# A deeper look ahead at the first double pair of each feed-forward

## The chip, the cores and the metric

One core of a Trainium2 chip runs the whole kernel. The metric is the device time in microseconds of one execution; the number given is the median of several runs. The engines named are TensorE (PE; its weight loads PEld), VectorE (DVE), ScalarE (ACT), GpSimd (POOL) and SyncE (SP), which here only issues transfers.

## The reference, cut to what matters

One decoder block on 512 tokens of width 1024, all in float32: a gated feed-forward, a token-mixing layer (pooling and dilated attention), a second gated feed-forward, each with a normalisation whose shift, scale and gate come from a small conditioning product.

```python
def swiglu(u, w_in, w_out):
    a, b = jnp.split(u @ w_in, 2, axis=-1)
    return (jax.nn.silu(a) * b) @ w_out

u = modulate(rmsnorm(h, g_norm_ffn1[l]), sh1, sc1)
h = h + 0.5 * gt1 * swiglu(u, w_ffn1_in[l], w_ffn1_out[l])
...
h = h + 0.5 * gt3 * swiglu(u, w_ffn2_in[l], w_ffn2_out[l])
return rmsnorm(h, g_final)
```

The hidden width is 2816, that is 22 tiles of 128; each needs two columns of tiles of `w_in`, one for `a` and one for `b`. The change lies in the two feed-forwards alone.

## The kernel before, in words

**Numbers in two parts.** Every weight and activation is held as a high part, rounded to the fast matmul type (`fp32r`), and a low part, the rest. A product is three matmuls: high by high, high by low, low by high (`mm3`, L356).

**Chunks.** The weights come in chunks, mostly 128 x 1024 numbers (512 KB). `plan` (L150) lists them in the order of use. SyncE loads a chunk into one of five buffers (`fetch`, L227; the names are raw, and X for the buffers that lie in another tile). Then ScalarE writes its high part to `whi` (L313) and VectorE the low part to `wlo` (L327). For some chunks (`self.outer`) the low part is made another way: ScalarE writes the negative of the rounded chunk to `wlo` (L309), and an accumulating transfer that GpSimd issues (L311) adds the chunk from HBM. `whi` and `wlo` are rings with room for seven chunks (RING, L121, a little over 7 x 1024 columns); `room` (L259) says whether a chunk fits beside those still in use.

**The look ahead.** Ahead of each chunk's matmuls, `look(n)` (L336) fetches what it has buffers for and splits chunks up to n places ahead, as far as the ring has room. The schedule is manual: each engine executes its instructions in exactly the order in which this Python code issues them, so where `look` stands, and how far it looks, fixes where a piece stands among ScalarE's and VectorE's other work.

**The feed-forward.** Its first hidden tiles are computed plainly (`ffn_pair`, L710, and, in the second feed-forward, written out in `ffn2`, L928): one tile for `a`, one for `b`, each 8 x 3 matmuls on one chunk. From hidden tile 8 on (first feed-forward) or 4 on (second), two hidden tiles at a time are made by a scheme of seven products of half-size blocks in place of eight: the double pair, `duo` (L773). Some of its chunks are differences of loaded ones (`make`, L246, VectorE, L252), and some of its inputs sums of activations (the tiles S). Between its products ScalarE copies partial sums out of the accumulation banks (L776) and takes the silu (L794). The first double pair of each feed-forward also calls `first` behind its first product, which makes the last sum (L733 on ScalarE, L736 on VectorE) and then gives a buffer free. The second matrix is applied in the same way, four hidden tiles at a time: `out_quad` (L869), with its own copies on ScalarE (L873) and sums of hidden activations made by `h_sums` (L843: VectorE L853 and L859, ScalarE L856), which `later` and `step` drop in between the double pair's products. Both loops count seven products; a product here is 24 matmuls of 256 columns.

In the first feed-forward the order is: plain tiles 6 and 7, the double pair of 8 and 9, a quad, two double pairs, a quad, and so on. In the second: plain tiles 0 to 3, the double pair of 4 and 5, a quad, and so on. Look-ahead before: 4 in the last plain tiles, 3 to 5 within the first double pair, 5 in all later double pairs and quads.

Of the kernel before, what the change touches and what calls it, by code (L numbers as in the profile page):

```python
# [125 lines left out]
PLAIN = {0: 8, 2: 4}  # L126
# [16 lines left out]
class Kernel:  # L143
# [272 lines left out]
    def beside(self, j, i):  # L416

        if self.nh == 4 and j > PLAIN[0] and i in (2, 5):
            self.bg()
# [290 lines left out]
    def ffn_pair(self, j, beside=lambda: None):  # L710
        ahead = 3 + (j + 2 >= PLAIN[0])
        pa = self.ffn_tile(ahead)
        beside()
        s = self.ffn_silu(j, pa)
        pb = self.ffn_tile(ahead)
        beside()
        self.ffn_post(j, s, pb)

# [54 lines left out]
    def duo(self, j, first, last):  # L773

        nc, v = self.nc, self.nc.vector
        copy = lambda o, x: nc.scalar.activation(o, x, AF.Copy)  # L776
        T1, T2 = slice(0, HT), slice(HT, T)
        blk = lambda ks, t: [(self.UH[k][:, t], self.UL[k][:, t]) for k in ks]
        lo4, hi4 = range(4), range(4, 8)
        S = []  # L780
        for i in range(3):
            h, l = self.S[i]
            S.append([(h[:, k * HT:(k + 1) * HT], l[:, k * HT:(k + 1) * HT]) for k in range(4)])
        S.append(blk(lo4, T2))
        A, B, C = self.nb(), self.nb(), self.nb()
        s = self.fw.tile([P, 2 * T], F32, name="sl")
        q = lambda x: x.rearrange("p (j h t) -> p j h t", j=2, h=2)
        r = lambda x: x.rearrange("p (j t) -> p j t", j=2)
        u3 = r(self.fw.tile([P, T], F32, name="u3"))
        c = self.kept[j // 2 % 3]  # L790
        c0, c1 = q(c)[:, :, 0, :], q(c)[:, :, 1, :]
        ts = slice(0, 1 if j % 4 == 0 and j < PARTS[-1][0] else 2)
        HHp, HLp = (q(x) for x in self.hpair(j))
        silu = lambda h, bank: nc.scalar.activation(q(s)[:, :, h, :], r(bank), AF.Silu)  # L794

        def mult():
            v.tensor_tensor(c, s, c, op=OP.mult)

        def high():
            copy(HHp[:, :, ts, :], q(c)[:, :, ts, :])  # L800

        def low():
            v.tensor_tensor(HLp[:, :, ts, :], q(c)[:, :, ts, :], HHp[:, :, ts, :], op=OP.subtract)


        for i, (bank, u, start) in enumerate(((A, blk(lo4, T1), True), (B, S[0], True), (A, S[1], False),
                                              (C, blk(hi4, T1), False), (A, S[2], False), (B, S[3], False),
                                              (A, blk(hi4, T2), False))):
            if i == 6:
                v.tensor_tensor(c1, c1, u3, op=OP.add)  # L810
            self.look(3 + i // 3 if first else 5)
            self.product(bank, u, start)
            self.step()
            if i == 0:
                copy(C, A)
                if first:
                    first()
                    self.free.append(self.rawx[0])
            elif i == 1:
                copy(c1, r(B))  # L820
            elif i == 2:
                copy(c0, r(A))
            elif i == 3:
                silu(0, C)
            elif i == 4:
                copy(u3, r(A))
            elif i == 6:
                silu(1, A)
                v.tensor_tensor(c0, r(B), c0, op=OP.add)
            self.beside(j, i)  # L830
            if self.nh == 4 and j > PARTS[-1][0] and self.todo:
                self.todo.pop(0)()
        if last:
            mult()
            high()
            low()
        else:
            self.later(1, mult)
            n = 8 if self.nh == 4 and j % 4 == 0 else 2
            self.later(n, high)  # L840
            self.later(n, low)
# [86 lines left out]
    def ffn2(self):  # L928
        self.put, self.now = [], 0
        bk = [self.nb() for _ in range(4)]  # L930
        self.head(2, bk, AF.Silu)
        self.open_G()
        self.todo, last = self.u_steps(2)
        do = lambda n: [self.todo.pop(0)() for _ in range(n)]
        do(3)
        for j in range(2):
            self.ffn_post(j, self.ffn_silu(j, bk[2 * j]), bk[2 * j + 1], lambda low: (do(1), low()))
        pa = self.ffn_tile()
        do(len(self.todo))
        self.free.append(self.rawx[1])  # L940
        due = []
        self.ffn_post(2, self.ffn_silu(2, pa), self.ffn_tile(), due.append)
        pa = self.ffn_tile(4)
        due.pop()()
        self.ffn_post(3, self.ffn_silu(3, pa), self.ffn_tile(4), lambda low: self.later(1, low))
        self.ffn(2, 4, last)

    def open_G(self):
# [779 lines left out]
```

## Time and profile before

| | us |
|---|---|
| median of 3 runs | 1002.2 (1002.18 to 1004.14) |
| the profiled execution | 1001.14 |
| its span, first to last instruction | 999.4 |
| TensorE busy | 984.8 |
| VectorE busy | 807.2 |
| ScalarE busy | 544.9 |
| granted TensorE clock, mean | 0.998 |

Times in rows of the profile are microseconds from the span's start. A row of the timeline gives start, duration, engine, line, operation, what it writes and reads, shapes, count, and in brackets the idle time of that engine ahead of it with what ended it. The ends of matmuls are modelled, their starts are measured. The first double pair of the first feed-forward starts at 125.83 (L769), its quad at 145.16 (L891); in the second feed-forward the quad starts at 722.11.

### The profile page before, as it was taken

The page shows a single profiled execution, that of the slowest core. Times are in us where ns is not written, and L with a number is a line of the kernel's source. Part 1 is how long each engine was busy: PE and PEld are TensorE (multiplying, and loading weights), DVE is VectorE, ACT ScalarE, POOL GpSimd, SP SyncE. Part 2 cuts the span into 40 slices and gives each one's busy share as a digit, 9 for nine tenths or more (in the row PEclk, how much of TensorE's full clock was granted, in tenths as well). Part 3 has the DMA queues.
Part 4 walks back from the last instruction along what each step waited for, and adds up shares of the span by engine and source line. Part 5 has one row for each costly group of instructions (what it writes and reads, how often), then busy time and mean ns, then how long its engine had stood idle before and what let it go on. Part 6 is the DMA issues. An engine that isn't in the chain of part 4 may idle for free.

```text
span 999.4 us, 17017 instructions
## 1 busy us (share of the span) xinstructions
PE 984.8 (99%) x6868; PEld 915.4 (92%) x6868; DVE 807.2 (81%) x1229; ACT 544.9 (55%) x824; POOL 67.0 (7%) x75
## 2 busy tenths in 40 slices
PE   8999999999999999999999999999999999999997
PEld 6888899999999999889988888898999999999996
DVE  6979979999996677879567777569798989989654
ACT  6453277786766443333414233465577868676652
POOL 0000001110110000007100000000010110010001
PEclk9999999999999999999999999999999999999999
DMA  9867567867857223123265774323376567567502
GB/s 338 278 212 251 190 169 211 222 184 216 241 126 198 89 78 106 57 92 125 77 235 185 266 267 133 96 73 106 111 169 192 143 171 179 156 151 204 137 17 85
DMA packets 49601, 163.29 MB, mean 163 GB/s; under 512 B 5617, under 2 KB 8945, under 8 KB 49522
## 3 DMA queue, kind: packets, MB, share of 16 engines
q1 hardware_dynamic: 42354, 137.95, 40.5%
q0 software_dynamic: 6480, 23.60, 14.2%
q8 instruction: 54, 0.88, 0.4%
q10 hardware_dynamic: 688, 0.66, 0.2%
q14 instruction: 25, 0.20, 0.1%
HBM read 159.41 MB, written 2.77 MB: 162 GB/s over the span
## 4 chain that ended last, share of the span: by engine, by line
PE 94%; DVE 3%; DMA 1%; ACT 1%; issue 1%; DVEq 0%; ACTq 0%; POOLq 0%
PE bank L358 13%; PE bank L359 13%; PE bank L360 13%; PE bank L771 10%; PE bank L769 10%; PE bank L770 10%; PE bank L891 4%; PE bank L893 4%; PE bank L892 4%; PE bank L1658 2%; PE bank L1662 1%; PE bank L1660 1%; PE bank L1249 1%; DMA wlo<-wf1o 1%; PE bank L1430 1%; PE bank L1431 1%
## 5 line engine op out<-in xcount | busy, mean ns | idle before, releaser
L327 DVE TENSOR_TENSOR wlo<-raw,whi 128x1024 fp32r<-128x1024 f32 (+5 forms) x129 | 140.3, 1099 | 45.3 <-ACT whi L313 45.1
L313 ACT ACTIVATE whi<-raw 128x1024 fp32r<-128x1024 f32 (+5 forms) x157 | 148.1, 955 | 18.9 <-DMA raw<-wmix 6.3
L358 PE MATMUL bank<-UH,whi 128*128 128x512 f32 (+1 forms) x432 | 158.1, 366 | 0.0
L359 PE MATMUL bank<-UL,whi 128*128 128x512 f32 (+1 forms) x432 | 154.0, 357 | 0.1
L360 PE MATMUL bank<-UH,wlo 128*128 128x512 f32 (+1 forms) x432 | 153.9, 356 | 0.0
L771 PE MATMUL bank<-UH,wlo 128*128 128x256 f32 x512 | 141.4, 276 | 0.0
L769 PE MATMUL bank<-UH,whi 128*128 128x256 f32 x512 | 141.4, 276 | 0.0
L770 PE MATMUL bank<-UL,whi 128*128 128x256 f32 x512 | 141.4, 276 | 0.0
L769 PE MATMUL bank<-SH,whi 128*128 128x256 f32 x384 | 107.0, 279 | 0.0
L771 PE MATMUL bank<-SH,wlo 128*128 128x256 f32 x384 | 106.9, 278 | 0.0
L770 PE MATMUL bank<-SL,whi 128*128 128x256 f32 x384 | 106.8, 278 | 0.0
L313 ACT ACTIVATE whi<-X 128x1024 fp32r<-128x1024 f32 (+3 forms) x109 | 90.5, 854 | 20.8 <-DVE X L252 20.7
L770 PEld LDWEIGHTS bank<-UL,whi 128*128 128x128 f32 x512 | 96.2, 188 | 0.1
L769 PEld LDWEIGHTS bank<-UH,whi 128*128 128x128 f32 x512 | 96.1, 188 | 0.1
L327 DVE TENSOR_TENSOR wlo<-X,whi 128x1024 fp32r<-128x1024 f32 (+3 forms) x92 | 83.1, 927 | 16.1 <-ACT whi L313 16.0
L771 PEld LDWEIGHTS bank<-UH,wlo 128*128 128x128 f32 x512 | 96.1, 188 | 0.0
L360 PEld LDWEIGHTS bank<-UH,wlo 128*128 128x128 f32 x432 | 81.1, 188 | 12.1
L359 PEld LDWEIGHTS bank<-UL,whi 128*128 128x128 f32 x432 | 81.2, 188 | 11.8 <-issue 0.5
L358 PEld LDWEIGHTS bank<-UH,whi 128*128 128x128 f32 x432 | 81.2, 188 | 11.3 <-issue 0.5
L770 PEld LDWEIGHTS bank<-SL,whi 128*128 128x128 f32 x384 | 72.5, 189 | 0.0
L769 PEld LDWEIGHTS bank<-SH,whi 128*128 128x128 f32 x384 | 72.5, 189 | 0.0
L771 PEld LDWEIGHTS bank<-SH,wlo 128*128 128x128 f32 x384 | 72.4, 189 | 0.0
(340 smaller groups left out, 2402.5 us busy)
## 6 DMA issues: line engine op xcount, KB each, us to landing
ada<-wada SPq DMA_DIRECT2D x47, 512.0 KB, 5.3
raw<-wmix SPq DMA_DIRECT2D x43, 512.0 KB, 4.1
raw<-wf1i SPq DMA_DIRECT2D x32, 512.0 KB, 6.2
raw<-wf2i SPq DMA_DIRECT2D x30, 512.0 KB, 4.5
AR<-wada SPq DMA_DIRECT2D x16, 512.0 KB, 4.1
wlo<-wf2i POOLq DMA_DIRECT2D x16, 512.0 KB, 5.7
X<-wf2i SPq DMA_DIRECT2D x14, 512.0 KB, 5.2
raw<-wf1o SPq DMA_DIRECT2D x12, 512.0 KB, 5.0
```

The lines of the kernel that those rows point to most:

```text
L313: self.nc.scalar.activation(self.hi[:, y], r[:, x], AF.Copy)
L327: self.nc.vector.tensor_tensor(self.lo[:, y], r[:, x], self.hi[:, y], op=OP.subtract)
L358: M(ps, hi, uh, start=start, stop=False)
L359: M(ps, hi, ul, start=False, stop=False)
L360: M(ps, lo, uh, start=False, stop=stop)
L769: M(o, hi, uh, start=start and p == 0 and k == 0, stop=False, skip_group_check=True)
L770: M(o, hi, ul, start=False, stop=False, skip_group_check=True)
L771: M(o, lo, uh, start=False, stop=k == 3, skip_group_check=True)
L891: M(o, hi, uh, start=start and m % 2 == 0 and k == 0, stop=False, skip_group_check=True)
L892: M(o, hi, ul, start=False, stop=False, skip_group_check=True)
L893: M(o, lo, uh, start=False, stop=k == 1, skip_group_check=True)
L1658: M(b, hi, self.UH[k], start=k == 0, stop=False)
```

## The change

Three numbers that say how far ahead to look:

```diff
@@ ffn_pair
-        pb = self.ffn_tile(ahead)
+        pb = self.ffn_tile(ahead + (j + 1 == PLAIN[0]))
@@ duo
-            self.look(3 + i // 3 if first else 5)
+            self.look(5)
@@ ffn2
-        self.ffn_post(3, self.ffn_silu(3, pa), self.ffn_tile(4), lambda low: self.later(1, low))
+        self.ffn_post(3, self.ffn_silu(3, pa), self.ffn_tile(5), lambda low: self.later(1, low))
```

TensorE's and GpSimd's instructions stand as before. On ScalarE, VectorE and SyncE they are reordered, and the buffers that later chunks use change places. Three places show it.

ScalarE in the first double pair of the first feed-forward, as the difference (minus: before, plus: now); raw_66 and raw_67 hold the chunks of its products 4 and 5, X that of product 6, raw_68 the quad's first chunk, and the L776 are the copies behind products 0, 1 and 2:

```order
+L313 ACTIVATE whi<-raw_66 128x1024
 L676 ACTIVATE HI<-kept_123 128x256 x2
 L776 ACTIVATE bank_97<-bank_101 128x512
 L733 ACTIVATE UH<-X 128x4x256
-L313 ACTIVATE whi<-raw_66 128x1024
+L313 ACTIVATE whi<-raw_67 128x1024
 L776 ACTIVATE kept_122<-bank_102 128x2x256
-L313 ACTIVATE whi<-raw_67 128x1024
+L313 ACTIVATE whi<-X 128x1024
+L309 ACTIVATE wlo<-raw_68 128x1024
+L313 ACTIVATE whi<-raw_68 128x1024
 L776 ACTIVATE kept_122<-bank_101 128x2x256
```

Each chunk's piece has moved ahead of one copy: the quad's first chunk, L309, stood behind the third L776 and now stands ahead of it.

ScalarE at the seam from the last plain tile to the first double pair of the second feed-forward; L679 belongs to the plain tile, raw_68 is the chunk of product 4, raw_66 of product 5, cs of product 6:

```order
 L313 ACTIVATE whi<-X 128x1024
+L313 ACTIVATE whi<-raw_68 128x1024
 L679 ACTIVATE HI<-X 128x512
+L313 ACTIVATE whi<-raw_66 128x1024
 L776 ACTIVATE bank_102<-bank_100 128x512
 L733 ACTIVATE UH<-X 128x4x256
-L313 ACTIVATE whi<-raw_68 128x1024
+L313 ACTIVATE whi<-cs 128x1024
```

Here product 4's piece is issued within the plain tile, ahead of L679. In the first feed-forward, above, it stands behind the corresponding L679, because the ring had no room earlier.

VectorE in the first double pair of the second feed-forward, before, up to the difference L252 that makes the chunk for the quad's product 4 (L853 and L859 are the sums of hidden activations, L810 belongs to the double pair):

```order
L853 TENSOR_TENSOR cond<-cond 128x2x256
L859 TENSOR_TENSOR G<-X,ut 128x512
L327 TENSOR_TENSOR wlo<-X,whi 128x512 x2
L853 TENSOR_TENSOR cond<-X,cond 128x2x256
L859 TENSOR_TENSOR G<-cond,ut 128x512
L810 TENSOR_TENSOR AR<-AR,u_6364 128x2x256
L252 TENSOR_TENSOR X<-raw_68,X 128x1024
```

And now, from L736 to the same difference, here written to raw_68:

```order
L736 TENSOR_TENSOR UL<-X,UH 128x4x256
L327 TENSOR_TENSOR wlo<-cs,whi 128x1024
L252 TENSOR_TENSOR cs<-raw_68,raw_67 128x1024
L327 TENSOR_TENSOR wlo<-raw_67,whi 128x1024
L252 TENSOR_TENSOR X<-raw_66,cs 128x1024
L327 TENSOR_TENSOR wlo<-cs,whi 128x1024
L853 TENSOR_TENSOR X<-cond,X 128x2x256
L327 TENSOR_TENSOR wlo<-X,whi 128x512 x2
L853 TENSOR_TENSOR cond<-cond 128x2x256
L859 TENSOR_TENSOR G<-X,ut 128x512
L252 TENSOR_TENSOR raw_68<-raw_66,raw_68 128x1024
```

Between L736 and this difference stood 15 rows before and stand 9 now: two L327 and one L252 have moved ahead of L736, and L853, L859 and L810 now come behind the difference.

## The prediction

> **What bounds the kernel now.** I read the page first: the span, the busy times, and the chain of work that ended last.
>
> ```profile
> span 999.4 us, 17017 instructions
> ...
> PE 984.8 (99%) x6868; PEld 915.4 (92%) x6868; DVE 807.2 (81%) x1229; ACT 544.9 (55%) x824; POOL 67.0 (7%) x75
> ...
> PE 94%; DVE 3%; DMA 1%; ACT 1%; issue 1%; DVEq 0%; ACTq 0%; POOLq 0%
> ```
>
> TensorE is busy for 99% of the span and carries 94% of the chain. No instruction of it goes away here, so a change of order can win only what TensorE waits. Next I read the waits of TensorE alone. After the start-up only three are above 0.4 us:
>
> ```profile
> PE bank L893 <- DMA wlo<-wf1o: 1.3, 1, 1.3
> PE bank L891 <- ACT bank L873: 1.2, 1, 1.2
> PE bank L891 <- ACT sl L794: 0.7, 1, 0.7
> ```
>
> The timeline puts the first at the first quad of the first feed-forward, and the other two at the first quad of the second. "Product" below means one chunk's 24 matmuls; a duo has products 0 to 6, and so has the quad behind it.
>
> ```profile
> 145.16 0.28 PE L891 MATMUL bank<-HI,whi 128*128 128x256 f32 x1
> 145.27 0.28 PE L892 MATMUL bank<-HK,whi 128*128 128x256 f32 x1
> 146.84 0.38 PE L893 MATMUL bank<-HI,wlo 128*128 128x256 f32 x1 [1.29 <-DMA wlo<-wf1o]
> 147.06 0.28 PE L891 MATMUL bank<-HI,whi 128*128 128x256 f32 x1
> ...
> 726.08 0.28 PE L893 MATMUL bank<-ut,wlo 128*128 128x256 f32 x1
> 727.07 0.39 PE L891 MATMUL bank<-ut,whi 128*128 128x256 f32 x1 [0.71 <-ACT sl L794]
> 727.29 0.28 PE L892 MATMUL bank<-G,whi 128*128 128x256 f32 x1
> ...
> 728.47 0.28 PE L893 MATMUL bank<-ut,wlo 128*128 128x256 f32 x1
> 729.97 0.39 PE L891 MATMUL bank<-ut,whi 128*128 128x256 f32 x1 [1.22 <-ACT bank L873]
> 730.19 0.28 PE L892 MATMUL bank<-G,whi 128*128 128x256 f32 x1
> ```
>
> The first column is the start. Undisturbed, one matmul follows another after 0.11 (145.16 to 145.27). The bracket understates a stop, because ends are modelled; starts don't. First stop: 146.84 - 145.27 = 1.57, less 0.11, and 0.10 more at the restart (147.06 - 146.84 = 0.22 instead of about 0.12): 1.56. Second: 727.07 - 726.08 = 0.99, so 0.88 + 0.10 = 0.98. Third: 1.50, so 1.39 + 0.10 = 1.49. In all 1.56 + 2.47 = 4.03 us. That is all there is to win.
>
> **The change, first feed-forward.** The addition in the last plain tile (L715) does nothing here: in the order, product 4's piece stands behind the L679 that closes the last plain pair, so it is still issued inside the duo and not in the tile; the ring of seven chunks had no room for it earlier. What acts is the second edit: products 4 and 5 of the duo, product 6 and the chunks of the quad are split one product sooner. These rows carry the first stop:
>
> ```profile
> 126.75 0.63 ACT L679 ACTIVATE HI<-kept 128x512 fp32r<-128x512 f32 x1 [4.61 <-DVE kept L670]
> ...
> 129.41 1.05 ACT L733 ACTIVATE UH<-X 128x1024 fp32r<-128x1024 f32 x1
> ...
> 134.48 0.60 ACT L776 ACTIVATE kept<-bank 128x512 f32<-128x512 f32 x1 [1.19 <-PE bank L771]
> 134.97 1.05 ACT L313 ACTIVATE whi<-X 128x1024 fp32r<-128x1024 f32 x1
> 135.93 1.04 ACT L309 ACTIVATE wlo<-raw 128x1024 fp32r<-128x1024 f32 x1
> ...
> 151.24 1.06 ACT L873 ACTIVATE bank<-bank 128x512 f32<-128x512 f32 x2
> ...
> 130.49 1.22 DVE L736 TENSOR_TENSOR UL<-X,UH 128x1024 fp32r<-128x1024 f32 x1 [2.38 <-ACT UH L733]
> 131.64 1.22 DVE L327 TENSOR_TENSOR wlo<-raw,whi 128x1024 fp32r<-128x1024 f32 x1
> ...
> 137.30 1.00 POOL L311 DMA_DIRECT2D wlo<-wf1o x1 [136.86 <-DVE wlo L327]
> ...
> 137.30 9.49 DMA wlo<-wf1o
> ...
> 137.00 0.28 PE L769 MATMUL bank<-SH,whi 128*128 128x256 f32 x1
> ```
>
> The quad's first chunk gets its low part by an accumulating DMA from GpSimd. Its start follows the end of L309 (135.93 + 1.04 = 136.97) by 0.33. The page names VectorE's L327, which ended at the same moment. The transfer took 9.49. Today L309 stands behind the L776 of product 2, which waits for TensorE; the change puts it ahead of that.
>
> How early can it be? L733 starts at 129.41 as before, L736 at 130.49 as before. Behind it VectorE now does L252 for product 6 at once: 130.49 + 1.15 = 131.64, done at about 132.9. ScalarE then needs 0.96 for that chunk's whi (134.97 to 135.93) and reaches L309 at 133.9, done at 134.9; the DMA starts at 135.2 instead of 137.3, 2.1 earlier. With the same 9.49 it lands at 144.7. L893 wants it at 145.27 + 0.11 = 145.38, so it is 0.7 ahead and the 1.56 go. Bounds: all 1.56, or nothing if the transfer takes 11.6 or more; I take all, because the loads ahead of it move with it, so the nearest row is its own.
>
> What is late next? L776 of product 2 now waits behind three pieces (whi, wlo, whi: 132.9 + 3 x 0.96 = 135.8) and ends at 136.4 instead of about 135.1. Product 4, which writes the same bank, starts at 137.00: 0.6 to spare, bound 0 to 0.6 lost. The L873 pair would be late too: it begins at 151.24 and its first half ends at about 151.8, but product 2 of the quad, unstopped, starts at 145.16 + 2 x 2.72 = 150.6 (2.72 is a third of 137.00 to 145.16). It is covered today by the stop itself. But ScalarE's queue ahead of it moves too: L794 no longer has the last pieces in front of it and can go when product 6 ends (145.4), then two pieces (1.92), one half copy (0.5), then L873: done at about 148.9, 1.7 ahead.
>
> **The change, second feed-forward.** Both edits act: product 4 is split inside the plain tile, product 5 and the rest one product sooner. The rows:
>
> ```profile
> 721.64 1.04 ACT L313 ACTIVATE whi<-raw 128x1024 fp32r<-128x1024 f32 x1
> 724.95 1.06 ACT L313 ACTIVATE whi<-X 128x1024 fp32r<-128x1024 f32 x1 [2.27 <-DVE X L252]
> ...
> 726.44 0.58 ACT L794 ACTIVATE sl<-bank 128x512 f32<-128x512 f32 x1
> ...
> 729.33 1.06 ACT L873 ACTIVATE bank<-bank 128x512 f32<-128x512 f32 x2
> ...
> 707.45 1.23 DVE L736 TENSOR_TENSOR UL<-X,UH 128x1024 fp32r<-128x1024 f32 x1 [2.39 <-ACT UH L733]
> ...
> 723.03 0.69 DVE L810 TENSOR_TENSOR AR<-AR,u 128x512 f32<-128x512 f32 x1
> 723.63 1.22 DVE L252 TENSOR_TENSOR X<-raw,X 128x1024 f32<-128x1024 f32 x1
> ...
> 722.11 0.28 PE L891 MATMUL bank<-HI,whi 128*128 128x256 f32 x1
> ```
>
> Nothing is late as data. L794 reads what product 6 finished at about 722.3, yet starts at 726.44, because ScalarE keeps its order and stands 2.27 at a chunk (the quad's product 4) whose difference L252 VectorE ends only at 724.85. L873 is late behind L794. VectorE was idle 2.39 ahead of L736 and backed up after it.
>
> Changed: two L327 and one L252 go into those 2.39 and the idle stretch before it. From L736 (707.45, still released by L733) to the end of that L252 stand seven whole instructions and one in two halves, 1.15 each, and three half ones at 0.60: 8 x 1.15 + 1.8 = 11.0, so 718.5 instead of 724.85. Some 0.6 for waits between (L853 and L859 still need ScalarE's copies): 719.1. ScalarE does that whi by 720.2 and the half copy by 721, so L794 waits for TensorE alone: 722.3 to 722.9, wanted at 726.08 + 0.11 = 726.2. L873 then follows two pieces and a half copy: 722.9 + 1.92 + 0.5 = 725.3, done by 725.9, wanted when product 2 of the quad starts, 722.11 + 2 x 2.72 = 727.55. Margins 3.3 and 1.6: both stops go, 2.47. Bounds: 0 if VectorE is held over 3.3 longer, 2.47 otherwise.
>
> **After that** the gain must stay. The stage behind:
>
> ```profile
> 730.00:950.00 220.00, 220.00 (x1930) 220.00 (x1931) 192.64 (x234) 157.70 (x214) 19.12 (x22) 1.00 0.65 167
> ```
>
> Columns: window, sum, then TensorE, weight loads, VectorE, ScalarE and GpSimd busy, granted clock, DMA share, GB/s. TensorE has no hole in 220 us while VectorE is 88% and the DMA engines 65% busy, so everything there is paced by TensorE and moves with it. The renamed buffers (raw for X) change no count; cost 0, at most another wait of the sizes above.
>
> The sum: 1.56 + 2.47 = 4.03 from a profiled execution of 1001.14 (999.4 of span and 1.74 around it): 997.1. The median of the runs is 1002.2, 1.06 above it, so on their scale 1002.2 - 4.0 = 998.2.
>
> **Rivals.**
>
> *The DMA eats its head start.* The loads of the quad's matrices are pulled forward as well and run on the same engines. Then the first stop stays, only the second feed-forward gains, and the time is 1002.2 - 2.5 = 999.7. For it: 9.49 is the longest of all these transfers (landing times of the DMAs of L311).
>
> ```profile
> DMA to landing us min/median/max: 5.3/5.7/9.5
> ```
>
> Against it: the loads in front shift by the same 2 us. [...] Chance 0.14.
>
> *It does not do what it says.* The ring refuses the deeper look, as it does in the first feed-forward's plain tile. Then it is 1002.2. The order speaks against it: the pieces do move. Chance, with small losses elsewhere that cancel the gain, 0.15.
>
> *Slower: a load holds VectorE.* The differences for the quad's products 1 and 2 now stand on VectorE ahead of the sums and copies that TensorE needs, and they wait for fresh loads. In the first stage the first of these loads goes out when product 4's L327 has freed its buffer: L679 at 126.75, half a microsecond later the whi of 1.05, then L327 of 1.22, so about 129.7. VectorE comes to it after L252, two L327 and a short pair, 131.64 + 3 x 1.15 + 0.7 = 135.8. So a load costs nothing up to 6 us. The second goes out when L736 is done, 131.7, and is wanted at 137.0. Had it taken 9.5, VectorE would be 4.2 late: 141.2, then L252, L327 and L853 (1.2 + 1.2 + 0.6), ScalarE's half copy and L776 (0.5 + 0.6) end at 145.4, and product 6 (145.16 - 2.72 = 142.44) starts 3.0 late. In the second stage the same chain starts from a load at about 706.7 and ends near 720.3, 0.9 after product 6 (719.39) wants it. 3.0 + 0.9 is just what the stops give back; from 9.5 us on the change loses. At 11 us it is 4.5 + 2.4 - 4.0 = +2.9, 1005.1. Loads issued at this place took, with the DMA engines idle before (share 0.02, the last but one column):
>
> ```profile
> 129.00:132.00 3.00, 3.00 (x27) 3.00 (x26) 1.51 (x2) 2.67 (x4) 0.00 (x0) 1.00 0.02 5
> ...
> DMA to landing us min/median/max: 3.7/4.2/4.7
> ```
>
> 3.7 to 4.7 speak against it; the 9.49 of the accumulating one a little later is all that speaks for it. Chance 0.07.
>
> **The numbers.** Forecast 0.64, DMA rival 0.14, no effect 0.15, slower 0.07. About 0.2%, 2.0 us, is what a measurement can tell from no change. The first two lie over 2 us below, so faster 0.64 + 0.14 = 0.78; within 0.15; slower 0.07. Range: the low end is the profiled scale, 997.1; the high end takes in no effect, 1002.3; left out are the slower case and a little below.
>
> **What would show it.** Right: in the profile after, the three waits of TensorE are gone from its list; the first DMA of GpSimd starts near 135.2 and lands before 145.4; L794 of the second stage's first duo starts near 722.3 and its L873 near 725.3; the span is about 995.4. Wrong: L893 at the first quad still waits for wlo; L769 at product 4 or 6 of a first duo waits for L776; or VectorE's L252 there waits for a load longer than 1 us.

## The result, and the profile after

| | before | after |
|---|---|---|
| median of the runs | 1002.2 (6 runs, 1000.6 to 1004.1) | 997.5 (6 runs, 996.9 to 1000.8) |
| profiled execution: time, span | 1001.14, 999.4 | 998.64, 996.7 |
| first duo to next duo, first feed-forward | 39.95 | 38.36 |
| first duo to next duo, second feed-forward | 40.91 | 38.37 |

The ratio of the times is 0.9958, with a 95% interval of 0.9941 to 0.9975. Runs of one kernel differ by up to 6 us, so what is below about 1 us is read from the traces. The last two rows of the table are the time from the start of the first duo's first matmul to the start of the duo behind the quad: 1.59 and 2.54 less, 4.13 in all. Forecast were 1.56 and 2.47.

The page of after, its span, the busy times and the chain that ended last:

```profile
span 996.7 us, 17019 instructions
...
PE 985.5 (99%) x6868; PEld 917.4 (92%) x6868; DVE 807.1 (81%) x1229; ACT 543.6 (55%) x824; POOL 68.2 (7%) x75
...
PE 96%; DVE 2%; DMA 1%; ACT 0%; issue 0%; SPq 0%; DVEq 0%; ACTq 0%
```

All that TensorE still waits for in after, from its list of waits:

```profile
PE bank L1580 <- ACT cond L1578: 3.3, 1, 3.3
PE bank L449 <- ACT ut L516: 0.3, 1, 0.3
PE bank L1618 <- DVE r L1615: 0.2, 1, 0.2
PE bank L1226 <- ACT prob L1214: 0.2, 1, 0.2
```

The waits of L893 for wlo (1.3) and of L891 for L873 (1.2) and L794 (0.7) are not on it. The 3.3 belongs to the start-up and was there before. At the three places TensorE's timeline of after runs on:

```profile
146.12 0.28 PE L892 MATMUL bank<-HK,whi 128*128 128x256 f32 x1
146.23 0.28 PE L893 MATMUL bank<-HI,wlo 128*128 128x256 f32 x1
...
724.54 0.28 PE L893 MATMUL bank<-HI,wlo 128*128 128x256 f32 x1
724.66 0.28 PE L891 MATMUL bank<-ut,whi 128*128 128x256 f32 x1
...
727.26 0.28 PE L893 MATMUL bank<-ut,wlo 128*128 128x256 f32 x1
727.38 0.28 PE L891 MATMUL bank<-ut,whi 128*128 128x256 f32 x1
```

From 146.12 to 146.23, from 724.54 to 724.66 and from 727.26 to 727.38: the step of an undisturbed stream, where 1.57, 0.99 and 1.50 stood.

The profiled span fell by 2.7 and not by 4.1. Of the difference 0.9 lies in the first 60 us, and 0.6 between 360 and 376 (last section). This is after's row of busy times there; the granted clock, the last column but two, was 1.00 in before:

```profile
0.00:60.00 60.00, 56.45 (x250) 46.43 (x251) 48.19 (x90) 30.50 (x42) 0.20 (x4) 0.97 0.86 306
```

3.4 us of it ran at half the clock (0.50 from 15 to 17), and the first duo starts at 126.68 instead of 125.83. So 0.85 is to be taken off after's times in the first feed-forward when they are set beside the forecast.

### The profile page after: what moved, and what is told of

Its sections match the earlier page's. It is cut to its first block, busy times and chain, and to the rows that moved or that the text cites. A ratio compares the mean times of both kernels' runs of the same rounds, so it can differ in the third digit from the quotient of the medians.

```text
span 996.7 us, 17019 instructions
## 1 busy us (share of the span) xinstructions
PE 985.5 (99%) x6868; PEld 917.4 (92%) x6868; DVE 807.1 (81%) x1229; ACT 543.6 (55%) x824; POOL 68.2 (7%) x75
## 4 chain that ended last, share of the span: by engine, by line
PE 96%; DVE 2%; DMA 1%; ACT 0%; issue 0%; SPq 0%; DVEq 0%; ACTq 0%
PE bank L358 13%; PE bank L359 13%; PE bank L360 13%; PE bank L769 10%; PE bank L770 10%; PE bank L771 10%; PE bank L892 4%; PE bank L891 4%; PE bank L893 4%; PE bank L1658 1%; PE bank L1660 1%; PE bank L1662 1%; PE bank L1249 1%; PE bank L1430 1%; PE bank L1431 1%; PE bank L1432 1%
## 5 line engine op out<-in xcount | busy, mean ns | idle before, releaser
L327 DVE TENSOR_TENSOR wlo<-raw,whi 128x1024 fp32r<-128x1024 f32 (+5 forms) x130 | 140.7, 1092 | 44.8 <-ACT whi L313 44.5
L358 PE MATMUL bank<-UH,whi 128*128 128x512 f32 (+1 forms) x432 | 158.3, 366 | 0.0
L360 PE MATMUL bank<-UH,wlo 128*128 128x512 f32 (+1 forms) x432 | 154.1, 357 | 0.0
L327 DVE TENSOR_TENSOR wlo<-X,whi 128x1024 fp32r<-128x1024 f32 (+3 forms) x91 | 81.4, 917 | 15.6 <-ACT whi L313 15.6
L360 PEld LDWEIGHTS bank<-UH,wlo 128*128 128x128 f32 x432 | 81.3, 188 | 12.1
L358 PEld LDWEIGHTS bank<-UH,whi 128*128 128x128 f32 x432 | 81.2, 188 | 11.2 <-issue 0.5
```

The source lines that it names most:

```text
L327: self.nc.vector.tensor_tensor(self.lo[:, y], r[:, x], self.hi[:, y], op=OP.subtract)
L358: M(ps, hi, uh, start=start, stop=False)
L360: M(ps, lo, uh, start=False, stop=stop)
```

## The experiments

**One half alone, then the other.** The first run has the first feed-forward as after and the second as before:

```diff
@@ duo, from after
-            self.look(5)
+            self.look(3 + i // 3 if first and self.nh == 6 else 5)
@@ ffn2
-        self.ffn_post(3, self.ffn_silu(3, pa), self.ffn_tile(5), lambda low: self.later(1, low))
+        self.ffn_post(3, self.ffn_silu(3, pa), self.ffn_tile(4), lambda low: self.later(1, low))
```

> The first feed-forward as after, the second as before. Theory (the gain is TensorE's three stops, and they add): the wait of L893 for wlo is gone, the two waits of L891 in the second feed-forward stay at 0.7 and 1.2 in the list; from duo start to duo start 38.36 in the first stage as after and 40.91 in the second as before; 1.6 less than before, 1000.6. Rival (the stops hang together: shifting the first moves where the second falls, or a part of the 4.7 between the medians comes from elsewhere in the program): the second feed-forward takes neither 40.9 nor 38.4, or the time is nearer to 997.5 or to 1002.2 than to 1000.6.

The second has it the other way round:

```diff
@@ ffn_pair, from after
-        pb = self.ffn_tile(ahead + (j + 1 == PLAIN[0]))
+        pb = self.ffn_tile(ahead)
@@ duo
-            self.look(5)
+            self.look(3 + i // 3 if first and self.nh == 4 else 5)
```

> The second feed-forward as after, the first as before. Theory (three stops that add): the 1.3 of L893 for wlo stays, both waits of L891 are gone, 39.95 from duo start to duo start in the first stage and 38.37 in the second; 2.5 less than before, 999.7. Together with the other half this must give the whole: 1.6 + 2.5 = 4.1 of the 4.7 between the medians. Rival (a part of the gain lies outside the two stages): the two halves together fall short of the whole by 0.5 or more.

Measured: 1000.57 and 999.24, beside 1001.75 for before on the same chip. The waits of TensorE in the first of the two:

```profile
PE bank L891 <- ACT bank L873: 1.2, 1, 1.2
PE bank L891 <- ACT sl L794: 0.7, 1, 0.7
```

and in the second:

```profile
PE bank L893 <- DMA wlo<-wf1o: 1.4, 1, 1.4
```

From duo to duo the two stages took 38.37 and 40.90 in the first run, 40.04 and 38.37 in the second. Each half removes its own stops and leaves the others as they were. 1.2 + 2.5 = 3.7 against 4.0 for the whole on that chip (997.78, next run): the stops add, as far as runs can tell whose gains are uncertain by 1.3 either way. In the two halves the times from duo to duo agree with those of before and after to 0.1.

**Which of the three numbers acts.** Two more runs on the same chip, each with one edit taken back:

```diff
@@ ffn_pair, from after (the first of the two)
-        pb = self.ffn_tile(ahead + (j + 1 == PLAIN[0]))
+        pb = self.ffn_tile(ahead)
@@ ffn2, from after (the second)
-        self.ffn_post(3, self.ffn_silu(3, pa), self.ffn_tile(5), lambda low: self.later(1, low))
+        self.ffn_post(3, self.ffn_silu(3, pa), self.ffn_tile(4), lambda low: self.later(1, low))
```

> After without the edit in the last plain tile of the first feed-forward (L715). Theory (that edit moves nothing, since the ring has no room there): the same instructions in the same order, 997.5 within what a measurement varies, up to 1 either way. Rival (it does act): a piece on ScalarE moves back across L679, and the GpSimd transfer starts later than 136.0; up to the 1.4 by which the low part is ahead this costs nothing, beyond that the first stop comes back in part.

> After without the deeper look in the second feed-forward's last plain tile: the chunk of product 4 is split inside the first duo again, behind L679, and its VectorE half L327 behind L670; all later pieces stand as in after. Theory (VectorE has 0.5 to 1 us of idle time there, and L736 waits for L733 and not for pieces): all three stops stay gone, 997.5. Rival (VectorE is backed up from L736 on, so one L327 more costs its whole 1.15 at L252): L252 of the quad's product 4 ends at 720.2 instead of 719.1; L794 still waits for TensorE alone with 2.2 to spare and L873 comes 0 to 0.6 before it is wanted, so again about 997.5, but with L873 nearer to 726 than to 725.

Measured: 997.78 and 997.84. The first has after's instructions in after's order in both stages, on every engine, so the look of five in that plain tile does nothing. In the timeline of the second, VectorE's difference for the quad's product 4 and ScalarE's L794 behind it (the duo starts at 701.39):

```profile
717.89 1.22 DVE L252 TENSOR_TENSOR raw<-raw,raw 128x1024 f32<-128x1024 f32 x1
...
720.92 0.60 ACT L794 ACTIVATE sl<-bank 128x512 f32<-128x512 f32 x1 [0.19 <-PE bank L771]
```

In after, where the duo starts 1.2 later, that L252 starts at 717.88: here it comes 1.2 late, as the rival had it, since VectorE is backed up. But L794 still waits for TensorE, 0.19 where it waits 0.96 in after, and so nothing is lost. All of the gain comes from the look in the duo.

The first of the two runs is after a second time, and its trace shows what one profile of after could not. GpSimd's transfer and TensorE at the quad, in its timeline:

```profile
135.07 1.00 POOL L311 DMA_DIRECT2D wlo<-wf1o  x1 [134.63 <-ACT wlo L309]
...
145.11 0.28 PE L892 MATMUL bank<-HK,whi 128*128 128x256 f32 x1
145.27 0.38 PE L893 MATMUL bank<-HI,wlo 128*128 128x256 f32 x1
```

and how long that transfer took, from the profile's answer on the tile wlo (the time from issue to landing):

```profile
DMA to landing us min/median/max: 10.2/10.2/10.2
```

It landed at about 145.27, where L893 starts; L893 was due at 145.22 (145.11 + 0.11). A stop of 0.05 with a slow restart is left: that product took 2.89 instead of 2.72. In the profile of after, the same transfer and its time:

```profile
136.08 1.00 POOL L311 DMA_DIRECT2D wlo<-wf1o  x1 [135.63 <-ACT wlo L309]
```

```profile
DMA to landing us min/median/max: 8.7/8.7/8.7
```

It landed at 144.8, 1.4 ahead of 146.23. So that margin was 1.4 in one execution and nothing in another.

**Half the dose.** A look of four in products 0 to 5, both plain tiles as before:

```diff
@@ duo, from before
-            self.look(3 + i // 3 if first else 5)
+            self.look((4, 4, 4, 4, 4, 4, 5)[i] if first else 5)
```

> Half the dose: both first duos look four chunks ahead in products 0 to 5 and five in product 6, both plain tiles as before. Theory (the time is the sum of what each stop has left, by the engines' queues): in the first stage L309 stands directly behind the L776 of product 2 and starts 0.96 earlier than before, the transfer lands about 145.8 and 0.6 of the first stop stays; in the second, one L327 fewer stands between L736 and the L252 of the quad's product 4, which ends 1.15 earlier, 723.7: L794 is then just in time, and L873 leaves 1.3 of its stop. 1.0 + 1.2 gained: 1000.0, between 999.2 and 1000.4. Rival (all or nothing: what counts is whether the quad's chunk passes the L776 and L794 that wait for TensorE): the first stop stays whole, 1.5, since L309 stands behind the L776 as before: 1001 or more.

Measured: 997.61, as much as the whole. Neither the sum nor the all-or-nothing rival foresaw that. The time of the transfer in its trace, and in its timeline the L252, L873 and TensorE:

```profile
DMA to landing us min/median/max: 8.8/8.8/8.8
```

```profile
720.09 1.22 DVE L252 TENSOR_TENSOR raw<-X,raw 128x1024 f32<-128x1024 f32 x1
...
725.72 0.58 ACT L873 ACTIVATE bank<-bank 128x512 f32<-128x512 f32 x1
...
726.35 0.39 PE L891 MATMUL bank<-ut,whi 128*128 128x256 f32 x1
```

The transfer started at 136.16, close to the 136.3 of my working, but took 8.8 and not 9.5, so it was in time. In the second stage the L252 ended at 721.2, 19.9 after the duo's start at 701.30; in before it was 724.85 - 702.78 = 22.1. It gained 2.1, not the 1.15 of the one L327 less, because a wait of 0.93 that VectorE had in that row of before went too. From duo to duo the stages took 38.59 and 38.79, 0.2 and 0.4 over after, where I had 0.6 and 1.3. The 0.4 is what is left of the third stop. The 0.2 is not left over from the first: TensorE's timeline has it at product 2 of the quad (L893 at 150.29, the next L891 at 150.53), a wait for L873, which the stop itself covered in before.

**ScalarE's order, twice.** First before, with the pieces bunched up ahead of one copy:

```diff
@@ duo, from before
-            self.look(3 + i // 3 if first else 5)
+            self.look((5 if i == 2 and self.nh == 4 else 3 + i // 3) if first else 5)
```

> Before, but in the first feed-forward's first duo the look goes to five at product 2: the pieces of product 6 and of the quad's first chunk pass the L776 of product 2 all at once, while the earlier ones stay where they were. Theory (ScalarE keeps its order, so an L776 behind pieces that wait for VectorE makes TensorE wait): the L252 of product 6 still ends at 134.7, three pieces of 0.96 follow, L776 ends at 138.0 instead of 135.1 and product 4, due at 137.0, starts about 1.1 late; the transfer starts at 136.9 and lands in time for the shifted quad. The stop moves from the quad to product 4 and shrinks from 1.6 to 1.1: 1001.7. Rival (the copies have spare time enough, only the start of the transfer counts): no wait at product 4, 1.2 left at L893, 1001.8. The time doesn't tell these apart, the place of the wait does.

Measured: 1002.04, ratio to before 1.0002 (0.9988 to 1.0016). TensorE's list, and ScalarE's piece that set the end:

```profile
PE bank L891 <- ACT bank L873: 1.3, 1, 1.3
PE bank L769 <- ACT kept L776: 1.0, 1, 1.0
PE bank L891 <- ACT sl L794: 0.7, 1, 0.7
```

```profile
135.14 1.06 ACT L313 ACTIVATE whi<-X 128x1024 fp32r<-128x1024 f32 x1 [1.40 <-DVE X L252]
...
138.00 0.58 ACT L776 ACTIVATE kept<-bank 128x512 f32<-128x512 f32 x1
```

The stop went from the quad to product 4 of the duo: the L776 stands behind three pieces, and the first of them waits 1.40 for VectorE. Another 0.4 is lost at the restart and in the quad's products 1 and 2 (2.90 and 2.84 instead of 2.72), so nothing is won. The change differs in that the pieces of products 4 and 5 move as well. So VectorE starts the difference 5.80 behind the start of the duo (132.48 in after) and not 7.61 (133.89 here), and the three pieces are done before product 4 wants its bank.

Then after, with L309 of the quad's first chunk issued three times:

```diff
@@ split_hi, from after
-            for y, x in parts:
+            for y, x in parts * (3 if i == min(self.outer) else 1):
                 self.nc.scalar.activation(self.lo[:, y], r[:, x], AF.Copy, scale=-1.0)
```

> After, with the ScalarE copy L309 of the first quad's first chunk issued three times, the same result each time: 1.91 of ScalarE's time more, ahead of the L776 of product 2. Theory (that L776 had 0.66 to spare): it ends at about 139.1 and product 4 of the duo, due at 137.8, starts 1.3 to 1.5 late; the transfer starts 1.9 later, lands at 146.7, and the quad wants the low part at 146.2 + 1.4, so no second stop: 998.9. Rival A (the transfer is what is short: the 1.4 by which it was ahead is used up): L893 waits again, 0.5 or more, and the L776 doesn't count, 998.0. Rival B (ScalarE has slack of more than 2 us): 997.5.

Measured: 999.37, 1.8 over the 997.6 that after and the kernels equal to it took. ScalarE and product 4 in its timeline, and the time of the transfer, which was issued at 137.53:

```profile
133.96 3.24 ACT L309 ACTIVATE wlo<-raw 128x1024 fp32r<-128x1024 f32 x3
...
136.99 0.28 PE L771 MATMUL bank<-UH,wlo 128*128 128x256 f32 x1
138.68 0.38 PE L769 MATMUL bank<-SH,whi 128*128 128x256 f32 x1 [1.42 <-ACT kept L776]
```

```profile
DMA to landing us min/median/max: 8.0/8.0/8.0
```

The two extra copies take 3.24 - 1.05 = 2.2, and product 4 starts 1.58 late (138.68 - 136.99, less 0.11): 0.6 was spare, as forecast. The transfer started 2.5 later than in the second execution of after and landed at 145.5, only 0.3 later (the stage itself began 0.3 later).

**A load that holds VectorE.** The slower rival, forced in the first stage (this kernel's lines are 3 higher than after's):

```diff
@@ plan, from after
+        n = min(self.outer.values())
+        self.twice = (n + 1, n + 2)
@@ fetch
-            for c in self.pieces(i, w):
-                self.nc.sync.dma_start(self.buf[i][:, c], src[:, c])
+            for _ in range(2 if i in self.twice else 1):
+                for c in self.pieces(i, w):
+                    self.nc.sync.dma_start(self.buf[i][:, c], src[:, c])
```

> After, with the loads of the first quad's second and third chunk issued twice each (the same bytes to the same place): the rival of the prediction in which a load holds VectorE, forced. In after these loads took 4.0 and 3.6. Theory (VectorE keeps its order, so its L252 for the quad's products 1 and 2 hold the sums behind them): at the 211 to 234 GB/s moved here the second chunk lands near 141.8 instead of 136.2, its L252 starts 3.9 later than 137.9, the L853 and with it ScalarE's L776 behind it come late, and product 6 of the duo starts 2 to 3 late: 999.5 to 1000.5. Rival (VectorE has that much slack in this stage, or the transfer of the low part is what suffers first): no wait at product 6; if the low part's transfer is stretched by the 1 MB more, 4 to 5 us, L893 waits 3, 1000.5; if neither, 997.5.

Measured: 1006.30, ratio to before 1.0040 (1.0026 to 1.0054): slower than before. SyncE's issues of the third chunk, VectorE's L255 (L252 in after) and TensorE in its timeline, then two rows of its busy times, with the granted clock in the last column but two:

```profile
134.60 5.76 SPq L239 DMA_DIRECT2D X<-wf1o  x2
...
142.36 0.28 PE L774 MATMUL bank<-UH,wlo 128*128 128x256 f32 x1
...
144.45 1.23 DVE L255 TENSOR_TENSOR X<-X 128x1024 f32<-128x1024 f32 x1 [5.33 <-DMA X<-wf1o]
...
148.69 0.58 PE L772 MATMUL bank<-UH,whi 128*128 128x256 f32 x1 [6.05 <-ACT u L779]
```

```profile
145.00:146.50 1.50, 0.00 (x0) 0.00 (x0) 1.50 (x3) 0.79 (x1) 0.00 (x0) 0.58 1.03 423
...
150.00:152.00 2.00, 2.00 (x11) 2.00 (x11) 2.00 (x3) 2.00 (x4) 0.76 (x1) 0.50 0.27 29
```

The second issue of each load came 4.5 and 5.4 behind its first (SyncE's rows of two last 4.85 and 5.76, one issue 0.33), so the third chunk came at 144.4, 12.7 after the 131.7 at which the prediction had its load go out, and not at the 141.8 that I expected. By the prediction's working (3.0 late at 9.5, and 1 more for each further us) product 6 starts 6.2 late: it starts at 148.69, and was due 0.11 behind 142.36, which is 6.2. What the working lacked is the clock. It fell to 0.50 during the stop (0.58 over the first row means: at 145.2) and stayed there until about 152, and product 6 took 4.41 instead of 2.72: 1.7 more. 6.2 + 1.7 = 7.9; the span is 7.8 over that of the second execution of after (1003.2 and 995.4).

**Longer stops.** The same repeated L309, five times and seven:

```diff
@@ split_hi, from after
-            for y, x in parts:
+            for y, x in parts * (5 if i == min(self.outer) else 1):
```

> After, with the L309 of the first quad's first chunk issued five times: 3.82 of ScalarE more ahead of the L776 of product 2. Theory (a stop costs its own length as long as the granted clock stays at 1.0; where L309 stood three times, 1.91 more gave a stop of 1.58 and 0.13 at the restart): the stop at product 4 is 3.5, and 0.1 at the restart, no half clock behind it: 997.6 + 3.6 = 1001.2. Rival (any stop of some us drops the clock, as the 6.1 did where the loads were issued twice: 0.5 for 6.8 us, of which 3.3 fell on matmuls and cost 1.7): 1002.9.

> After, with that L309 issued seven times: 5.73 more. [...]

Measured: 1004.92 (1002.0 to 1008.2, 10 runs) and 1005.85 (1004.9 to 1008.2, 7 runs). With five that is above what I expected; the rival, a drop of the clock, is what the trace shows, though its 1002.9 is too low as well. TensorE's timeline and two rows of busy times, with five:

```profile
136.22 0.28 PE L771 MATMUL bank<-UH,wlo 128*128 128x256 f32 x1
140.10 0.58 PE L769 MATMUL bank<-SH,whi 128*128 128x256 f32 x1 [3.60 <-ACT kept L776]
```

```profile
138.00:142.00 4.00, 1.90 (x9) 1.90 (x10) 1.31 (x3) 4.00 (x7) 1.00 (x1) 0.74 0.48 115
142.00:146.00 4.00, 4.00 (x31) 4.00 (x31) 4.00 (x6) 2.49 (x4) 0.00 (x0) 0.84 0.90 199
```

A stop of 3.77, and behind it half the clock for another 3.2, until 143.3 (0.84 over the second row); product 4 took 4.36 instead of 2.72. With seven the stop is 5.96 and the product takes 4.40. That makes 5.4 and 7.6 of the 7.3 and 8.2 by which the medians rise over 997.6. Of the ten times with five, four lie at 1002.0 to 1003.0 with a mean granted clock of 0.995 to 0.996, the profiled one among them, and six at 1004.6 to 1008.2 with 0.992 to 0.994. The trace explains the first four; where the other six lost more of the clock isn't shown. With seven, 997.6 and the stop alone make 1003.6: all 7 runs lie above that, at 1004.9 or more. There the clock fell 2.4 after TensorE's last matmul (at 139.9, by the row below; that matmul starts at 137.45), with the loads issued twice 2.8 after it, with five 3.6 after it:

```profile
138.00:144.00 6.00, 0.48 (x2) 0.48 (x3) 1.07 (x2) 5.90 (x8) 1.00 (x1) 0.66 0.18 68
```

A fixed idle time doesn't fit three different delays. What sets the moment of the drop isn't shown.

**The loads beside the transfer.** In the traces of before and after and of the first six runs the transfer lands 0.1 to 0.8 ahead of the second of two loads that run beside it. (Where L309 is repeated it lands 0.2 to 1.3 behind it, which the expectation below overlooks.) The last run cuts both to an eighth of their columns (a part of the first feed-forward is then computed on other numbers):

```diff
@@ plan, from after
+        n = min(self.outer.values())
+        self.cut = (n + 4, n + 5)
@@ fetch
-            for c in self.pieces(i, w):
+            for c in [slice(0, w // 8)] if i in self.cut else self.pieces(i, w):
```

> After, with the two loads that run beside the first quad's accumulating transfer (the first two chunks of the duo behind that quad) cut to an eighth of their columns; the rest of these chunks is whatever the buffer holds, so a part of the first feed-forward's product is computed on other numbers, in the same instructions. In the runs so far the transfer took between 7.2 and 10.2 and landed 0.1 to 0.8 ahead of the second of these loads, wherever it started. Theory (it shares the DMA engines with them, and they set when it lands): it takes 5.3 to 6.5, like those with little beside them, and lands 3 or more before L893 wants it. Rival (its time is its own, or comes of the loads ahead of it): 8.5 or more still. The time stays that of after in both, 997.6.

Measured: 998.21, as after. The transfer, issued at 135.15, took

```profile
DMA to landing us min/median/max: 8.0/8.0/8.0
```

Neither the 5.3 to 6.5 of the theory nor quite the 8.5 or more of the rival. With whole loads the same start gave 10.2 and 9.8 (the two kernels with one edit taken back), 8.7 (after) and 8.5 (the first half alone). So this one execution lies 0.5 to 2.2 below them; but where L309 stood three times the transfer took 8.0 with whole loads too, so a lengthening by the loads isn't shown. Nor do the cut loads land early: with an eighth of the bytes the second, issued at 137.04, took 6.3 and landed at 143.3, again 0.2 behind the transfer. That the two land together therefore doesn't show that the loads set the transfer's time. What fills its 8 us stays open.

## Why the prediction came out right, step by step

*TensorE's stops are all there is to win.* Shown: the halves remove exactly their stops (38.4 against 40 and 40.9 from duo to duo) and add up to the whole. 1.56 was 1.59 and 2.47 was 2.54.

*The first addition does nothing in the first feed-forward.* Shown by leaving it out (997.78). That "both edits act" in the second feed-forward holds for the order, not for the time: without the deeper plain tile it is 997.84.

*The first stop.* The start was right: 135.2 forecast, 136.08 less 0.85 is 135.2. The landing was right by luck as much as by reason. I took the transfer's 9.49 as fixed and had 0.7 to spare; it took 8.7, 10.2, 9.8 and 8.5 in the four kernels with this order there (after, the two with one edit taken back, the first half alone). And its start counts for less than I thought. SyncE's load beside the transfer is issued in before at

```profile
136.20 0.43 SPq L236 DMA_DIRECT2D X<-wf1i  x1
```

and where L309 stood three times at

```profile
134.50 0.42 SPq L236 DMA_DIRECT2D X<-wf1i  x1
```

The duos of these two start within 0.1 of each other and the transfers within 0.23 (137.30 and 137.53). The transfer landed at 146.8 in before and at 145.5 there, with the load 1.7 earlier. This would fit if the loads that the change pulls forward were a part of the gain, besides the transfer's own start; one pair of executions, with the scatter above, doesn't show it. The prediction had them as an argument ("the loads in front shift by the same 2 us"), not as a cause.

*The rival that the DMA eats the head start* was partly true. In the second execution of after (the kernel without the plain tile's edit) the transfer took 10.2, 0.7 longer than the 9.5 of before, and 0.15 of the stop was left: from L892 at 145.11 past L893 at 145.27 to the next L891 at 145.49 it is 0.38 instead of 0.23. In after, with 8.7, nothing was left (146.12 to 146.23). 8.0 stands both with the loads cut and, where L309 was issued three times, with whole ones, so what lengthens the transfer isn't shown by any run here.

*What is late next.* L776 of product 2 was to have 0.6 to spare. In after its row and product 4's are

```profile
136.60 0.58 ACT L776 ACTIVATE kept<-bank 128x512 f32<-128x512 f32 x1
...
137.84 0.28 PE L769 MATMUL bank<-SH,whi 128*128 128x256 f32 x1
```

0.66, and the repeated L309 shows it from the other side: 2.2 more of ScalarE made 1.58 of a stop.

*The second stage.* Forecast were 719.1, 722.3 and 725.3 for the end of L252 and the starts of L794 and L873:

```profile
707.28 1.23 DVE L736 TENSOR_TENSOR UL<-X,UH 128x1024 fp32r<-128x1024 f32 x1 [0.30 <-ACT UH L733]
...
717.88 1.22 DVE L252 TENSOR_TENSOR raw<-raw,raw 128x1024 f32<-128x1024 f32 x1
...
722.14 0.60 ACT L794 ACTIVATE sl<-bank 128x512 f32<-128x512 f32 x1 [0.96 <-PE bank L771]
...
725.05 1.07 ACT L873 ACTIVATE bank<-bank 128x512 f32<-128x512 f32 x2
```

L252 ended at 717.88 + 1.15 = 719.0, L794 and L873 began at 722.14 and 725.05, in a stage that began 0.17 earlier than in before. The idle 2.39 ahead of L736 is 0.30, L794 waits for TensorE alone, and both stops are gone. Counting VectorE's rows from L736 to that L252, with a fixed time for each, was enough here. In the half dose the same counting was off by 1, because I left the waits in the row where they were.

*The slower rival* had the right price for the stop itself (6.2 for a load of 12.7), but in that stop the clock also fell, to 0.50, 1.7 more. At the break-even that I gave, 9.5 us, the stop would be 3.0; whether the clock already falls there wasn't tried, though it fell 2.4 and 2.8 into two of the longer stops. The loads here took 3.6 and 4.0, so it never came near.

*The time.* 998.2 forecast from stops of 4.03; measured 997.5, 4.7 below before. The traces account for 4.13 of it; the other 0.6 is within what the medians vary (before had 1002.2, 1001.75, 1001.9, 1002.0 and 1002.3 in the five groups of runs).

## What to carry to other kernels

Where one engine is busy for 99% of the span, add up its stops from the starts of its instructions: that sum is the gain to be had (4.03 forecast, 4.13 in the traces), and each stop can be tried alone. When a piece is moved ahead of a copy on an engine that keeps its order, write down the new end of that copy and of what feeds the piece; moving only the last pieces moved the stop and won nothing (1002.04), moving the whole row of pieces won it all (997.5). Don't take a transfer's duration in one execution as fixed: here the same one took from 8.5 to 10.2, which is 1.7 us, more than the margin of 0.7.

## What the runs showed of the hardware

**Stops of TensorE of 3.8 us and more cost more than their length here.** Stops of 0.9 to 1.6 (the three of before, and L309 three times) cost their length and about 0.1 at the restart. After stops of 3.8, 6.0 and 6.2 (L309 five and seven times, the loads issued twice) the granted clock was 0.50 and the next product took 4.36 to 4.41 instead of 2.72, 1.6 to 1.7 more, because the half clock lasted another 3.2 to 3.4 behind the restart. Between 1.6 and 3.8 nothing was tried. Half the clock lasted 3.4 in all with five, and 6.8 with seven and with the loads issued twice; it began 3.6, 2.4 and 2.8 after the last matmul. One stretch of 3.4 us at half the clock also stands in the first 60 us of after's profile (0.91 from 10 to 15, 0.75 from 15 to 20) and not of before's (1.00).

**The same stream of matmuls has two speeds at full clock.** After the stop with five L309 the clock was back at 1.00, yet a matmul followed the other after 0.12 and not after 0.113:

```profile
150.11 0.28 PE L891 MATMUL bank<-HI,whi 128*128 128x256 f32 x1
150.23 0.28 PE L892 MATMUL bank<-HK,whi 128*128 128x256 f32 x1
```

A product then takes 2.827 instead of 2.720, up to the end of that quad, about 1 us in all. The same happens without a stop of that kind: in after's profile the stream of L358 to L360 ran at the slower step from about 360 to 376, where before ran at the faster one, and lost 0.6. What switches it isn't shown by any run here.
